# Gate and up products in a PSUM tile each: a two-layer hybrid trunk on one Trainium2 core

## The chip, the cores and the metric

The kernel runs on one core of a Trainium2 chip (trn2). The metric is the device time of one execution in microseconds, and the median of several executions is what is compared. The engines of the core are named as in the profile: PE (matrix products; PEld is its loading of stationary operands), DVE (VectorE), ACT (ScalarE), POOL (GpSimd) and SP, whose queue issues nearly all loads. Matrix products are accumulated in PSUM, from which ACT and DVE read.

## What is computed

Two layers run over 256 latent tokens and 256 context tokens of 1024 features in fp32. Each layer is a token mixer (two attentions and a convolution between an input and an output projection) followed by a mixture of experts; the second layer's mixture runs on the 256 latent tokens alone. The change lies in the experts:

```python
def hierarchical_moe(h, w_group, b_group, w_expert, b_expert, w_gate, w_up, w_down):
    # 32 experts in 4 groups; each token goes to 2 experts of one group
    ...
    def run(args):
        xb, e = args
        return (jax.nn.silu(xb @ w_gate[e]) * (xb @ w_up[e])) @ w_down[e]
    ...
```

with `w_gate` and `w_up` of 1024 x 512 and `w_down` of 512 x 1024 for each of 32 experts and each of two layers.

## The kernel before

**Experts.** A layer works through its 32 experts in 16 pairs, two of them to a quad `qd`. Each expert of a pair has 64 places for tokens, so that a pair fills the 128 PSUM partitions: expert `e` writes partitions 64e to 64e+63. `pair` (line 1344) does, in this order: 16 gate products (`m == 0`), the SiLU of their sum on ACT (`sil`, L1358), 16 up products (`m == 1`), the product of their sum with `sil` and the token weights on DVE (`act`, L1363), four transposes (`pat`), 16 down products into `py`, and `split_y`, which reads `py` in two halves: ACT rounds a half to `YH` (L1275), DVE subtracts to get the rest `YL` (L1276). In the second layer DVE first multiplies by a gate (`Yg`, L1273). The trace counts each of these fp32 products as two instructions, so its rows show 32 where the code has 16.

**Work between the products.** `burst(0)` stands between gate and up products, `burst(1)` behind `act`, `burst(2)` behind the transposes' copy, `burst(3)` amid the down products. They hold what belongs to neighbouring pairs: the return of the previous pair's rows to their tokens (`pc`, the "adders"), the gathering of the next quad's rows (`pg`) and its one-hot matrix `OH` (DVE, L1289). In the first layer, in all but the first and the last two pairs, `burst(0)` holds at most that one-hot matrix, which is no PE work. In the second layer it holds three adders from the second pair on.

**PSUM.** `ps2` has two places of two banks (2 x 512 fp32 for each partition), `ps1` four places of one bank. Before, a pair takes one place for gate and up together, `p[:, 0]` and `p[:, 1]`, and the other for `py`. A place is handed out in turn, and a program that orders instructions by what tiles they touch puts in the waits; it tracks whole tiles.

**Loads.** Weights come over SP's queue in loads of 1024 KB into a ring of eight slots: a pair needs twelve (four each for gate, up and down). A load waits on SP until the products that read its slot are done, so PE's progress sets when loads start. The first pairs of a layer read weights that were loaded during the mixer, and the last pair uses loads of half the size.

**Order.** SP's order is that of the code. PE, DVE and ACT follow the code in the expert pairs (`tc.manual_schedule`). In the second layer's mixer, between the two mixtures, a list scheduler that estimates durations for the whole program from its start chooses the order on PE and ACT, and on DVE in parts.

Of the kernel before, what the change touches and what calls it, by code (L numbers as in the profile page):

```python
# [14 lines left out]
AF = mybir.ActivationFunctionType  # L15
OP = mybir.AluOpType
# [20 lines left out]
def trunk(ctx: ExitStack, tc: tile.TileContext, t_in, rope, out, cfg):  # L37
    nc = tc.nc
    pe, ve, sc, gp, sp = nc.tensor, nc.vector, nc.scalar, nc.gpsimd, nc.sync
# [17 lines left out]
    def K2(name, shape=(128, 512), dt=F32, tag="t"):  # L57
        t = k2[tag].tile([shape[0], 256 if tag == "m" else 512], dt, tag="k2" + tag, name=name)
        n = int(np.prod(shape[1:]))
        t = t[:, :n]  # L60
        if len(shape) == 3:
            t = t.rearrange("p (a b) -> p a b", a=shape[1])
        elif len(shape) == 4:
            t = t.rearrange("p (a b c) -> p a b c", a=shape[1], b=shape[2])
        return t

    def P2(name, dt=F32):
        return ps2.tile([128, 2, 512], dt, tag="p2", name=name)

    def P1(name, dt=F32):  # L70
        return ps1.tile([128, 512], dt, tag="p1", name=name)
# [29 lines left out]
    def load_rows_two(srcs, name):  # L101

        vs = [slot(name).rearrange("p (k f) -> p k f", f=512) for _ in srcs]
        for b in range(2):
            for v, src in zip(vs, srcs):
                sp.dma_start(v[:, 2 * b:2 * b + 2], src[b] if isinstance(src, list) else src[:, 2 * b:2 * b + 2])
        return [lambda k, v=v: v[:, k] for v in vs]
# [104 lines left out]
    def sqrt_table(after):  # L212

        sc.activation(sm.tile([128, 1], F32, name="warm"), after[:, 0:1], AF.Sqrt, scale=0.0)
# [249 lines left out]
    def layer(l):  # L464
# [39 lines left out]
        if l > 0:  # L504
            ws = Splits(wKV, 512)
# [486 lines left out]
        def down_half(h, e, pr):  # L992
            return [wdown_d[l, 2 * pr + e][256 * a:256 * a + 256, 512 * h:512 * h + 512].rearrange("(p k) d -> p k d", k=2)
                    for a in range(2)]
# [3 lines left out]
        def weights_of(pr, m, a, e):  # L998
            return down(a, e, pr) if m == 2 else gate_up(m, a, e, pr)
# [242 lines left out]
        def row_adders(YH, YL, oht, new=P1):  # L1242

            def d_major(o):
                pc = new("pc")
                pe.matmul(pc, YH[:, 128 * o:128 * o + 128], oht, start=True, stop=False)  # L1246
                pe.matmul(pc, YL[:, 128 * o:128 * o + 128], oht, start=False, stop=True)  # L1247
                for s in range(2):
                    sl = slice(256 * s, 256 * s + 256)
                    ve.scalar_tensor_tensor(xT[:, o, sl], pc[:, sl], mod[l][:, 5, o, s:s + 1], xT[:, o, sl],  # L1250
                                            op0=OP.mult, op1=OP.add)

            def t_major(t, hf):
                pc = new("pc")
                o_, sl = oht[:, 128 * t:128 * t + 128], slice(512 * hf, 512 * hf + 512)
                pe.matmul(pc, o_, YH[:, sl], start=True, stop=False)  # L1256
                pe.matmul(pc, o_, YL[:, sl], start=False, stop=True)  # L1257
                ve.tensor_tensor(xo[t][:, sl], xo[t][:, sl], pc, op=OP.add)  # L1258

            if last:  # L1260
                return [lambda t=t, hf=hf: t_major(t, hf) for hf in range(2) for t in range(2)]
            return [lambda o=o: d_major(o) for o in range(KC)]

        def y_tiles():
            return K4("YH", (128, 1024), F32R), K4("YL", (128, 1024), F32R), K4("Yg") if last else None

        def split_y(py, h, rows, tiles):

            YH, YL, y = tiles
            sl = slice(512 * h, 512 * h + 512)  # L1270
            py = py[:rows]
            if last:
                ve.tensor_tensor(y[:rows, sl], py, g2r[:rows, sl], op=OP.mult)  # L1273
                py = y[:rows, sl]
            sc.copy(YH[:rows, sl], py)  # L1275
            ve.tensor_tensor(YL[:rows, sl], py, YH[:rows, sl].bitcast(F32), op=OP.subtract)  # L1276
# [59 lines left out]
        def weight(m, a, e, pr):  # L1336

            t = pre.pop((pr, m, a, e), None) or load_rows(weights_of(pr, m, a, e), "we")
            if not isinstance(t, list):
                return lambda k: t[:, k]  # L1340
            n = 1 if m == 2 else 2
            return lambda k: t[k // n][:, k % n]

        def pair(pr, xg, ws, burst, final, finish):


            p = P2("pgu")
            for m in range(2):
                for a in range(2):
                    w_ = (load_rows_two([weights_of(pr, m, a, e) for e in range(2)], "we") if final else  # L1350
                          [weight(m, a, e, pr) for e in range(2)])
                    for k in range(4 * a, 4 * a + 4):
                        for e in range(2):
                            pe.matmul(p[64 * e:64 * e + 64, m, :], xg[:, k, 64 * e:64 * e + 64], w_[e](k % 4),  # L1354
                                      start=k == 0, stop=k == KC - 1)
                if m == 0:
                    sil = K2("sil", tag="w")
                    sc.activation(sil, p[:, 0], AF.Silu)  # L1358
                    if final:
                        sqrt_table(sil)  # L1360
                    burst(0)
            act = K2("act", tag="w")
            ve.scalar_tensor_tensor(act, p[:, 1], ws, sil, op0=OP.mult, op1=OP.mult)  # L1363
            burst(1)
            pt = P1("pat")
            for f in range(4):
                pe.transpose(pt[:, 128 * f:128 * f + 128], act.rearrange("s (a p k) -> s a k p", a=2, k=2)[:, f // 2, f % 2], ident)  # L1367
            actT = K2("actT", tag="w")
            sc.copy(actT, pt)  # L1369
            burst(2)  # L1370
            tiles = y_tiles()
            oht = K2("oht", (128, 512), F32R)

            def slots():
                pb = P1("pb")
                se = sm.tile([32, 2, 64], F32R, name="se")
                gp.tensor_copy(se, ident[:32, 2 * pr:2 * pr + 2, None].to_broadcast([32, 2, 64]))  # L1377
                pe.matmul(pb[:, :N], se.rearrange("p a b -> p (a b)"), posT[:, :N], start=True, stop=True)  # L1378
                ve.tensor_scalar(oht[:, :N], pb[:, :N], slotid, None, op0=OP.is_equal)

            def products(py, wd, fs):
                for f in fs:
                    for e in range(2):
                        pe.matmul(py[64 * e:64 * e + 64, :], actT[:, 128 * f + 64 * e:128 * f + 64 * e + 64],  # L1384
                                  wd[e](f), start=f == 0, stop=f == 3)

            slots()
            if final:
                for h in range(2):
                    py = P2("py")[:, 0]  # L1390
                    wd = load_rows_two([down_half(h, e, pr) for e in range(2)], "we")
                    products(py, wd, range(2))
                    if h == 0:
                        burst(3)
                    else:
                        finish(0, tiles, oht[:, :N], py)
                    products(py, wd, range(2, 4))
                    if h == 0 or not last:
                        split_y(py, h, 128, tiles)
                finish(1, tiles, oht[:, :N], py)  # L1400
                return []
            py = P2("py")
            for a in range(2):
                wd = [weight(2, a, e, pr) for e in range(2)]
                for f in range(2 * a, 2 * a + 2):
                    for h in range(2):
                        for e in range(2):
                            pe.matmul(py[64 * e:64 * e + 64, h], actT[:, 128 * f + 64 * e:128 * f + 64 * e + 64],  # L1408
                                      wd[e](f % 2)[:, 512 * h:512 * h + 512], start=f == 0, stop=f == 3)
                if a == 0:  # L1410
                    burst(3)
            for h in range(2):
                split_y(py[:, h], h, 128, tiles)
            return row_adders(tiles[0], tiles[1], oht[:, :N])
# [183 lines left out]
        for qd in range(8):  # L1598
            nxt, steps, _ = quad(qd + 1) if qd < 7 and (qd or cfg["n0"]) else (None, [], None)
            for e in range(2):  # L1600
# [4 lines left out]
                with man():  # L1605
# [21 lines left out]
                    def burst(i):  # L1627
                        for f in at[i]:
                            f()
# [62 lines left out]
```

## Time and profile before

| | |
|---|---|
| Median of 3 executions | 1475.16 us (1473.77 to 1477.0) |
| The profiled execution, its own time | 1472.71 us |
| Its span, first to last instruction | 1470.7 us |
| Experts of the first layer | about 305 to 798 us |
| Mixer of the second layer | about 798 to 994 us |
| Experts of the second layer | about 994 to 1460 us |
| PE busy, share of the span | 95% |
| DVE, ACT busy | 42%, 27% |
| Moved from HBM | 479.42 MB, 327 GB/s over the span |

Times in rows are microseconds from the start of the span. "idle before" is how long the engine stood still ahead of an instruction, and the arrow names what ended that.

### The profile page before, as it was taken

The numbers are of one execution on the slowest core, as the hardware profiler recorded it, in microseconds if no ns is written. First come the engines' busy times: TensorE is split into PE (matmuls) and PEld (weight loads), VectorE is DVE, ScalarE is ACT, GpSimd is POOL, SyncE is SP. The second block draws the span as 40 slices with busy tenths as digits, with TensorE's granted clock in tenths as the row PEclk, the third lists the DMA queues.
The fourth block names the chain that finished last, engine by engine and source line by source line (L and its number), as shares of the span: only waits on it lengthen the run. The fifth ranks groups of instructions, "written<-read, shape, count | busy, mean of one in ns | idle before, by whom it ended". The sixth has DMA issues, their size and how long they took to land. (4 is left out here: it accounts for less than half of the span.)

```text
span 1470.7 us, 20485 instructions
## 1 busy us (share of the span) xinstructions
PE 1390.8 (95%) x8068; PEld 771.3 (52%) x8068; DVE 613.4 (42%) x1380; ACT 395.7 (27%) x954; POOL 76.7 (5%) x132
## 2 busy tenths in 40 slices
PE   6999999999999999999998998889999999999987
PEld 5776677755445544444434776783433343333332
DVE  4379974443323423233325679853222222222223
ACT  4454675421111111101102565552111011111102
POOL 1202000100000000000001110010000000000000
PEclk9999999999999999999999999999999999999999
DMA  9757204397999999999999590186999999999996
GB/s 350 282 166 284 109 1 172 131 375 306 376 408 414 413 400 406 417 406 414 385 405 389 201 332 31 44 357 280 388 422 421 421 421 421 421 421 419 421 417 255
DMA packets 97412, 481.86 MB, mean 328 GB/s; under 512 B 14068, under 2 KB 22544, under 8 KB 52128
## 3 DMA queue, kind: packets, MB, share of 16 engines
q1 hardware_dynamic: 96576, 478.79, 81.1%
q8 instruction: 66, 1.08, 0.3%
q10 hardware_dynamic: 464, 1.11, 0.2%
q0 software_dynamic: 272, 0.59, 0.1%
q14 instruction: 34, 0.28, 0.0%
HBM read 479.42 MB, written 1.05 MB: 327 GB/s over the span
## 5 line engine op out<-in xcount | busy, mean ns | idle before, releaser
L1354 PE MATMUL pgu<-we,xg 128*64 128x512 f32 x1904 | 449.3, 598 | 30.7 <-DMA we<-in_w_gate_dram 13.6
L1354 PEld LDWEIGHTS pgu<-we,xg 128*64 128x64 f32 x1904 | 142.3, 137 | 324.1 <-issue 246.8
L1408 PE MATMUL py<-we,actT 128*64 128x512 f32 x888 | 202.9, 596 | 0.7 <-ACT actT L1369 0.7
L1363 DVE SCALAR_TENSOR_TENSOR act<-pgu,ws,sil 128x512 f32<-128x512 f32 x32 | 24.0, 751 | 285.1 <-PE pgu L1354 248.6
L1250 DVE SCALAR_TENSOR_TENSOR xT<-pc,mod,xT 128x256 f32<-128x256 f32 x256 | 104.8, 477 | 52.9 <-PE pc L1247 52.2
L1408 PEld LDWEIGHTS py<-we,actT 128*64 128x64 f32 x888 | 63.1, 137 | 117.5 <-issue 113.4
L1304 ACT COPY xg<-pg 128x256 f32<-128x256 f32 x112 | 36.3, 376 | 308.2 <-PE pg L1300 308.2
L1258 DVE TENSOR_TENSOR xo<-xo,pc 128x512 f32<-128x512 f32 x62 | 39.8, 684 | 112.0 <-PE pc L1257 112.0
L1299 PE MATMUL pg<-OH,hH 128*128 128x256 f32 x336 | 83.3, 286 | 0.0
L1300 PE MATMUL pg<-OH,hL 128*128 128x256 f32 x336 | 82.1, 283 | 0.0
L643 DVE SCALAR_TENSOR_TENSOR ca<-gpad,cw,ca 128x512 f32<-128x512 f32 (+1 forms) x120 | 74.2, 619 | 0.9
L1299 PEld LDWEIGHTS pg<-OH,hH 128*128 128x128 f32 x336 | 63.9, 190 | 7.2 <-issue 5.7
L1300 PEld LDWEIGHTS pg<-OH,hL 128*128 128x128 f32 x336 | 64.1, 191 | 0.9
L1358 ACT ACTIVATE sil<-pgu 128x512 f32<-128x512 f32 x32 | 19.1, 598 | 167.6 <-PE pgu L1354 167.6
L281 PE MATMUL pm<-wm,scT 128*32 128x256 f32 (+1 forms) x896 | 60.7, 359 | 3.0 <-DMA wm<-in_w_mod_dram 2.8
L1273 DVE TENSOR_TENSOR Yg<-py,g2r 128x512 f32<-128x512 f32 x31 | 21.3, 688 | 100.7 <-PE py L1408 96.4
L1276 DVE TENSOR_TENSOR YL<-py,YH 128x512 fp32r<-128x512 f32 x32 | 22.1, 690 | 92.7 <-ACT YH L1275 92.7
L1275 ACT CAST YH<-Yg 128x512 fp32r<-128x512 f32 x31 | 19.1, 617 | 141.2 <-DVE Yg L1273 141.2
L1275 ACT CAST YH<-py 128x512 fp32r<-128x512 f32 x32 | 18.7, 585 | 139.0 <-PE py L1408 113.8
L1377 POOL CAST se<-ident 32x128 fp32r<-32x128 f32 x32 | 9.1, 287 | 900.1 <-PE pb L1378 900.1
L1246 PE MATMUL pc<-oht,YH 128*128 128x512 f32 x128 | 53.4, 418 | 1.2 <-ACT YH L1275 1.2
L1247 PE MATMUL pc<-oht,YL 128*128 128x512 f32 x128 | 50.6, 395 | 0.2 <-DVE YL L1276 0.2
(429 smaller groups left out, 2106.0 us busy)
## 6 DMA issues: line engine op xcount, KB each, us to landing
we<-in_w_up_dram SPq DMA_DIRECT2D x112, 1024.0 KB, 9.7
we<-in_w_down_dram SPq DMA_DIRECT2D x111, 1024.0 KB, 12.4
we<-in_w_gate_dram SPq DMA_DIRECT2D x110, 1024.0 KB, 13.5
wm<-in_w_mod_dram SPq DMA_DIRECT2D x44, 1024.0 KB, 9.4
wp<-in_w_gate_dram SPq DMA_DIRECT2D x8, 1024.0 KB, 9.5
wp<-in_w_up_dram SPq DMA_DIRECT2D x8, 1024.0 KB, 9.7
we<-in_w_gate_dram SPq DMA_DIRECT2D x16, 512.0 KB, 12.1
we<-in_w_up_dram SPq DMA_DIRECT2D x16, 512.0 KB, 10.2
```

What stands on the lines that cost most here:

```text
L281: pe.matmul(p[0][32 * q:32 * q + 32], scT[:, kq, :], ws[128 * kq // nr][:, kq % (nr // 128), c:c + n], start=k == 0, stop=k == KC * nq // ...
L643: ve.scalar_tensor_tensor(a, g, wt, a, op0=OP.mult, op1=OP.add)
L1246: pe.matmul(pc, YH[:, 128 * o:128 * o + 128], oht, start=True, stop=False)
L1247: pe.matmul(pc, YL[:, 128 * o:128 * o + 128], oht, start=False, stop=True)
L1250: ve.scalar_tensor_tensor(xT[:, o, sl], pc[:, sl], mod[l][:, 5, o, s:s + 1], xT[:, o, sl], op0=OP.mult, op1=OP.add)
L1258: ve.tensor_tensor(xo[t][:, sl], xo[t][:, sl], pc, op=OP.add)
L1275: sc.copy(YH[:rows, sl], py)
L1299: pe.matmul(dst, hH[t][:, 128 * k:128 * k + 128], rhs, start=t == 0, stop=False)
L1300: pe.matmul(dst, hL[t][:, 128 * k:128 * k + 128], rhs, start=False, stop=t == NT - 1)
L1304: sc.copy(xg[e][:, k - 1:k + 1, :], v[:, :, e])
L1354: pe.matmul(p[64 * e:64 * e + 64, m, :], xg[:, k, 64 * e:64 * e + 64], w_[e](k % 4), start=k == 0, stop=k == KC - 1)
L1408: pe.matmul(py[64 * e:64 * e + 64, h], actT[:, 128 * f + 64 * e:128 * f + 64 * e + 64], wd[e](f % 2)[:, 512 * h:512 * h + 512], start=f == ...
```

## The change

Gate and up products of a pair get a tile of `ps2` each, of which only the first bank is used, in place of the two banks of one tile. With `py` a pair now takes three tiles, and since there are two places, the three results of consecutive pairs take them by turns: gate in A, up in B, `py` in A, the next pair's gate in B, its up in A, its `py` in B. What a product waits for at its start is the reading of the tile that had its place before: a gate product's that of the previous pair's up result (`act`), an up product's that of the previous pair's `py` (`split_y`), a down product's that of its own pair's gate result (`sil`).

```diff
         def pair(pr, xg, ws, burst, final, finish):
 
 
-            p = P2("pgu")
             for m in range(2):
+                p = P2("pgu")[:, 0]
                 for a in range(2):
                     w_ = (load_rows_two([weights_of(pr, m, a, e) for e in range(2)], "we") if final else
                           [weight(m, a, e, pr) for e in range(2)])
                     for k in range(4 * a, 4 * a + 4):
                         for e in range(2):
-                            pe.matmul(p[64 * e:64 * e + 64, m, :], xg[:, k, 64 * e:64 * e + 64], w_[e](k % 4),
+                            pe.matmul(p[64 * e:64 * e + 64, :], xg[:, k, 64 * e:64 * e + 64], w_[e](k % 4),
                                       start=k == 0, stop=k == KC - 1)
                 if m == 0:
                     sil = K2("sil", tag="w")
-                    sc.activation(sil, p[:, 0], AF.Silu)
+                    sc.activation(sil, p, AF.Silu)
                     if final:
                         sqrt_table(sil)
                     burst(0)
             act = K2("act", tag="w")
-            ve.scalar_tensor_tensor(act, p[:, 1], ws, sil, op0=OP.mult, op1=OP.mult)
+            ve.scalar_tensor_tensor(act, p, ws, sil, op0=OP.mult, op1=OP.mult)
             burst(1)
```

On PE no product of the experts moves. What changes is what the first up product waits for. Here is that place in a pair of the first layer (the third row of the piece, in its two versions, is the first up product; DMAHW names a load, Activation is ACT):

```order
 L1354 MATMUL pgu<-we,xg 64x512 [waits DMAHW2_49]
 L1354 MATMUL pgu<-we,xg 64x512 x6
-L1354 MATMUL pgu<-we,xg 64x512 [waits DMAHW3_49,Activation_49]
+L1354 MATMUL pgu<-we,xg 64x512 [waits DMAHW3_49,DVE_49,PE_49]
 L1354 MATMUL pgu<-we,xg 64x512 [waits DMAHW4_49]
 L1354 MATMUL pgu<-we,xg 64x512 x6
```

The wait for ACT has gone, and waits for DVE (the reading of the previous `py`) and for PE's own earlier products have come.

The orders on SP and POOL stay. In the second layer's mixer, whose code the diff does not touch, the scheduler chooses another order on PE, ACT and DVE. On ACT, at the start of that mixer (`hT`: the modulated rows for the input projection, two instructions for each k; `wh`: rounding of its weights; `ms` and `mod`: a modulation vector), before:

```order
L352 COPY rs<-rb 128x512
L370 ACTIVATE hT<-hx,mod_224 128x256
L288 COPY ms<-pm 128x256
L370 ACTIVATE hT<-hx,mod_224 128x256 x3
L304 COPY mod_224<-pm 128x16
L370 ACTIVATE hT<-hx,mod_224 128x256 x2
L385 CAST wh<-wkv 128x512
```

and now:

```order
L352 COPY rs<-rb 128x512
L370 ACTIVATE hT<-hx,mod_224 128x256 x4
L288 COPY ms<-pm 128x256
L370 ACTIVATE hT<-hx,mod_224 128x256 x4
L304 COPY mod_224<-pm 128x16
L385 CAST wh<-wkv 128x512 x2
L370 ACTIVATE hT<-hx,mod_224 128x256
```

The copy `ms` moves behind three more `hT`, and two `wh` stand together. On DVE, at the end of that mixer's convolution (`ca`: a tap of the convolution; `ars`, `qT`: attention results; `wl`: the rest of the rounded weights; `csq`, `cn2v`, `cn2r`: the convolution's norm), before:

```order
L643 SCALAR_TENSOR_TENSOR ca<-gpad,cw,ca 128x256 x2
L387 TENSOR_TENSOR wl<-wo,wh 128x512
L643 SCALAR_TENSOR_TENSOR ca<-gpad,cw,ca 128x256 x2
L871 TENSOR_TENSOR ars<-po,ars 128x128
L786 TENSOR_TENSOR ca<-ca,cm 128x256 x2
L874 TENSOR_TENSOR qT<-ars,qT 128x128
L790 TENSOR_TENSOR csq<-csq,csq_8343 128x256
L330 TENSOR_SCALAR cn2v<-css 128x2
L387 TENSOR_TENSOR wl<-wo,wh 128x512
```

and now:

```order
L643 SCALAR_TENSOR_TENSOR ca<-gpad,cw,ca 128x256
L871 TENSOR_TENSOR ars<-po,ars 128x128
L387 TENSOR_TENSOR wl<-wo,wh 128x512
L874 TENSOR_TENSOR qT<-ars,qT 128x128
L786 TENSOR_TENSOR ca<-ca,cm 128x256 x2
L790 TENSOR_TENSOR csq<-csq,csq_8359 128x256
L387 TENSOR_TENSOR wl<-wo,wh 128x512
L330 TENSOR_SCALAR cn2v<-css 128x2
```

Three of the taps have moved to an earlier place in the mixer, and one `wl` stands ahead of `cn2v` in place of behind it.

## Rows read from the trace of the kernel before

**Rows 1.** The page of the profile: the span, PE's busy time, and what the loads moved in each of 40 slices of the span (about 37 us a slice).
```profile
span 1470.7 us, 20485 instructions
...
PE 1390.8 (95%) x8068; PEld 771.3 (52%) x8068; DVE 613.4 (42%) x1380; ACT 395.7 (27%) x954; POOL 76.7 (5%) x132
...
GB/s 350 282 166 284 109 1 172 131 375 306 376 408 414 413 400 406 417 406 414 385 405 389 201 332 31 44 357 280 388 422 421 421 421 421 421 421 419 421 417 255
```

**Rows 2.** PE's waits between 305 and 800 us (the first layer's experts), longest total first: total us, how often, the longest one.
```profile
PE pgu L1354 <- ACT sil L1358: 10.3, 13, 1.1
PE pgu L1354 <- DVEq L1454: 1.5, 1, 1.5
PE pc L1246 <- ACT YH L1275: 1.2, 1, 1.2
...
```

**Rows 3.** The timeline of all engines over one pair boundary of the first layer, from the down products of one pair to the first up products of the next: start, duration, engine, line, instruction, count. SPq is SP's queue issuing loads.
```profile
513.56 7.09 PE L1408 MATMUL py<-we,actT 128*64 128x512 f32 x32
...
517.24 4.24 SPq L98 DMA_DIRECT2D we<-in_w_up_dram  x4
520.48 7.04 PE L1354 MATMUL pgu<-we,xg 128*64 128x512 f32 x32
520.72 0.59 ACT L1275 CAST YH<-py 128x512 fp32r<-128x512 f32 x1 [8.21 <-PE py L1408]
...
522.07 0.59 ACT L1275 CAST YH<-py 128x512 fp32r<-128x512 f32 x1 [0.76 <-DVE YL L1276]
522.68 0.69 DVE L1276 TENSOR_TENSOR YL<-py,YH 128x512 fp32r<-128x512 f32 x1 [0.65 <-ACT YH L1275]
...
527.92 0.60 ACT L1358 ACTIVATE sil<-pgu 128x512 f32<-128x512 f32 x1 [5.27 <-PE pgu L1354]
528.58 0.65 PE L1354 MATMUL pgu<-we,xg 128*64 128x512 f32 x2 [1.06 <-ACT sil L1358]
```

**Rows 4.** PE's timeline: gate products (no wait) and up products (behind the wait) of three other pairs of the first layer; 397.21 and 644.03 are the gates of two pairs eight apart.
```profile
397.21 7.04 PE L1354 MATMUL pgu<-we,xg 128*64 128x512 f32 x32
405.03 7.09 PE L1354 MATMUL pgu<-we,xg 128*64 128x512 f32 x32 [0.78 <-ACT sil L1358]
...
551.13 7.04 PE L1354 MATMUL pgu<-we,xg 128*64 128x512 f32 x32
558.95 7.09 PE L1354 MATMUL pgu<-we,xg 128*64 128x512 f32 x32 [0.78 <-ACT sil L1358]
...
644.03 7.04 PE L1354 MATMUL pgu<-we,xg 128*64 128x512 f32 x32
```

**Rows 5.** DVE's timeline at the pair whose gate starts at 551.13: the last half of the split, late because a one-hot matrix went ahead of it.
```profile
553.74 0.68 DVE L1276 TENSOR_TENSOR YL<-py,YH 128x512 fp32r<-128x512 f32 x1
```

**Rows 6.** Two single microseconds of the pair boundary of rows 3: busy time of each engine, then PE's granted clock (1.00 is the upper level), the share of the 16 DMA engines' time, and GB/s.
```profile
517.00:518.00 1.00, 1.00 (x8) 0.38 (x6) 0.00 (x0) 0.00 (x0) 0.00 (x0) 1.00 0.59 246
518.00:519.00 1.00, 1.00 (x8) 0.33 (x6) 0.00 (x0) 0.00 (x0) 0.00 (x0) 1.00 0.73 147
```

**Rows 7.** The same columns for one stretch of 30 us in each layer's experts.
```profile
510.00:540.00 30.00, 28.94 (x148) 13.55 (x147) 8.59 (x20) 3.19 (x8) 0.29 (x1) 1.00 0.99 407
...
1210.00:1240.00 30.00, 28.38 (x129) 11.19 (x129) 7.29 (x14) 3.33 (x8) 0.29 (x1) 1.00 1.01 421
```

**Rows 8.** ACT's timeline: the SiLU of two pairs of the second layer that are six apart.
```profile
1138.28 0.60 ACT L1358 ACTIVATE sil<-pgu 128x512 f32<-128x512 f32 x1 [5.84 <-PE pgu L1354]
...
1318.12 0.60 ACT L1358 ACTIVATE sil<-pgu 128x512 f32<-128x512 f32 x1 [6.24 <-PE pgu L1354]
```

**Rows 9.** The loads issued between 500 and 560 us (two pairs): count, KB each, median us from issue to landing.
```profile
we<-in_w_gate_dram SPq DMA_DIRECT2D x8, 1024.0 KB, 13.7
we<-in_w_up_dram SPq DMA_DIRECT2D x8, 1024.0 KB, 7.7
we<-in_w_down_dram SPq DMA_DIRECT2D x8, 1024.0 KB, 10.7
```

**Rows 10.** PE's waits between 1000 and 1470 us (the second layer's experts), as rows 2.
```profile
PE pgu L1354 <- DMA we<-in_w_gate_dram: 13.6, 14, 1.3
PE pgu L1354 <- DMA we<-in_w_up_dram: 3.0, 11, 0.3
...
PE pgu L1354 <- ACT sil L1358: 0.2, 1, 0.2
```

**Rows 11.** PE's waits between 795 and 1000 us (the second layer's mixer), as rows 2, the longest three.
```profile
PE pqt L734 <- DVE tq L731: 3.3, 1, 3.3
PE cr L344 <- DVE cn2r L338: 2.5, 1, 2.5
PE pp L1204 <- DVE selb L1193: 2.4, 1, 2.4
...
```

**Rows 12.** The first stretch of that mixer, columns as in rows 6.
```profile
806.00:892.00 86.00, 85.19 (x627) 64.50 (x629) 59.57 (x139) 46.46 (x115) 13.33 (x18) 0.98 0.70 253
```

**Rows 13.** Four rows of timelines of that mixer: three of the `hT` on ACT, taps on DVE, `cn2v` on DVE, and the first load for the second layer's experts on SP's queue.
```profile
811.66 1.31 ACT L370 ACTIVATE hT<-hx,mod 128x256 fp32r<-128x256 f32 x3
...
896.89 2.04 DVE L643 SCALAR_TENSOR_TENSOR ca<-gpad,cw,ca 128x256 f32<-128x256 f32 x4
...
950.56 0.34 SPq L1021 DMA_DIRECT2D xs<-in_w_down_dram  x1
...
952.48 0.16 DVE L330 TENSOR_SCALAR cn2v<-css 128x2 f32<-128x2 f32 x1 [0.76 <-PE css L423]
```

## The prediction, made before the changed kernel was run

> **What bounds the kernel now.** I read the page first, to see where PE and the loads are full, then PE's waits by stage, then the timeline of one pair boundary, and last the loads by the microsecond. PE is busy 95% of the span, and in the two expert stages the loads run at 375 to 422 GB/s in nearly every slice [rows 1]. Two limits lie close together, so each layer has to be read by itself.
>
> In the first layer's experts PE waits 10.3 us, 13 times, for the SiLU on ACT, then 1.5 us once for a branch; no load is among its longest waits [rows 2]. PE sets the pace there. One boundary shows why: the down products start at 513.56 and the gate products at 520.48, 6.92 us for 32 instructions without a gap; the up products start at 528.58, 8.10 us after the gate products, behind an ACT instruction that reads the tile's other half [rows 3]. In the usual pair it is 7.82 us (397.21 to 405.03, 551.13 to 558.95) with 0.78 us shown as idle [rows 4]. So a wait costs 7.82 - 6.92 = 0.90 us, 0.12 more than the idle that the profile shows, since the pipeline also drains. The period of a pair is (644.03 - 397.21) / 8 = 30.85 us [rows 4].
>
> In the second layer's experts PE waits 13.6 and 3.0 us for loads and 0.2 us for the SiLU, once [rows 10]: three adders stand between gate and up and hide it. The loads set the pace, with 421 GB/s [rows 7] and a period of (1318.12 - 1138.28) / 6 = 29.97 us [rows 8].
>
> **The change, part by part.**
>
> The wait removed: an up product no longer waits for `sil`, as its tile is another one. 13 waits of 10.3 us in all [rows 2], and 0.12 us of drain for each: 10.3 + 13 x 0.12 = 11.9 us. In the second layer it removes 0.2 us from PE, at a place where the first pair's weights are there already; I count it at nothing, since the loads set the end of that stage (if I am wrong, it is 0.2 us more).
>
> The wait added on up: it now waits for the split of the previous pair's `py`. In rows 3 the last `YL` ends at 522.68 + 0.69 = 523.37, 2.9 us after the gate products began; at the pair with a one-hot matrix ahead of it, 553.74 + 0.68 = 554.42, 3.3 us after 551.13 [rows 4, 5]. The gate products take 6.92 us, so 3.6 us are spare and the wait costs nothing. Without that cover (a split that ended only with the gate products) each further microsecond would cost a microsecond for each of the 13 pairs. Behind the waiting up product stand all PE's later products, so there is no way round it.
>
> The waits added on gate and down: gate waits for the previous `act`, down for its own pair's `sil`. The `sil` of rows 3 starts at 527.92 and is over some 15 us before that pair's down products (its up products alone take 7 us and the bursts follow); `act` lies a whole set of down products (6.92 us) ahead of the next gate. Nothing for both.
>
> What the loads then allow: a pair reads 12 loads of 1024 KB, 12.58 MB, or 29.9 us at 421 GB/s; the second layer, paced by its loads, does it in 29.97 [rows 8]. PE's new period in the first layer is 30.85 less 0.93 (the mean over these 8 pairs: seven of 0.90, one of 1.18) = 29.92 us. The two limits meet. Can the loads give this? Today the queue runs dry once a pair: up loads are issued at 517.24, when the down products have freed their slots [rows 3], and in the two microseconds from 517 the rate is 246 and 147 GB/s, in place of 421 [rows 6]: (175 + 274) / 421 = 1.07 us of a pair are lost. That is the room which the faster PE uses. The stock ahead of PE: the four up loads of a pair come in two groups, 7.7 us being their median to landing [rows 9]; issued at 517.24 and about 521, the second group lands about 529 and is needed halfway through the up products, near 527.5 + 3.5 = 531. That leaves about 2 us. If the loads lag by 29.97 - 29.92 = 0.05 us a pair, nine pairs use up 0.5 us of it. So I take the full gain up to the last pairs. There the half-size loads follow without a dry stretch, and the gain of the last of the 13 pairs (0.9 us) may go to a wait for them. Lower bound of this term: 11.9 - 0.5 - 0.9 = 10.5; upper bound 11.9; I take 11.3, nearer the upper, since rows 2 show no wait for a load at all today.
>
> A rule stands against this. The Trainium skill, in "TensorE: Matmul & The Clock Gate", section "HAM oscillation — how this bites in real kernels", reports a kernel whose products wait for transfers, and in which double buffering of PSUM "gave no further gain". By it the sum would be about nothing. The second layer here is that case (its row shows 0.2 us to win); the first, where PE waits for ACT and not for loads, is not.
>
> The order in the second layer's mixer: the scheduler sees the pairs end at other times and lays out about 200 us anew. Same instructions, same loads. On ACT `ms` stands behind three more `hT`, 1.31 us [rows 13]; PE meanwhile has products without a gap, 85.19 us of 86 [rows 12], which cover it; without the cover it would cost 1.3. On DVE three taps (2.04 us for four, so about 1.5 us) move away from the end of the convolution, whose norm PE waits 2.5 us for today [rows 11, 13]; a gain of up to 1.5 us at that place, paid for by attention steps that come as much later. `wl` ahead of `cn2v` lies in 0.76 us in which DVE waits for PE [rows 13]. Bounds: a loss of 1.3 + 1.5 = 2.8, a gain of 2.5 (the wait for the norm); I take 0.
>
> What carries it to the end: the first load of the second layer's experts is issued at 950.56, during that mixer [rows 13], and waits for attention's end; so the loads that pace the second layer start as much earlier as the mixer does, and what the first layer wins arrives whole.
>
> Sum: 1472.7 (the profiled execution's own time, 2.4 us under the median of the runs) - 11.3 = 1461.4; on the median 1475.2 - 11.3 = 1463.9 us, 0.77% faster.
>
> **The rivals.**
>
> (a) The loads don't give more in the first layer than they do now. For: 407 GB/s at a DMA share of 0.99 [rows 7], hence 12.58 / 407 = 30.9 us a pair, the present period. Against: the dry stretch of rows 6, and 421 in the second layer. Then only the first three pairs gain, which read preloaded weights: 3 x 0.9 = 2.7 us, 1472.5. It would show as waits of PE for up loads. This is the case in which the rule above would hold.
>
> (b) The mixer's new order costs 3 to 8 us. For: PE waits there for DVE and ACT in turn [rows 11], and its granted clock is not at the upper level all the time (mean 0.98) [rows 12]. Against: unchanged work and its long gapless stretch. Time 1467 to 1472, around 1469.
>
> (c) Slower: the split comes late, and up waits longer for DVE than it did for ACT. It decides once the last `YL` ends over 6.92 + 0.90 = 7.8 us after the gate's start, where it is 2.9 to 3.3 now. If the split of some 2.9 us ran only behind the gate products, up would start after 9.8 us in place of 7.8: 2.0 us for 15 pairs of the first layer, 30 us, 1505. Against: ACT and DVE are idle for 5 us ahead of `sil` [rows 3].
>
> (d) The wait doesn't go, since another wait on ACT stands in the same place: 1475. Against: the order of waits in the changed program.
>
> **How the numbers follow.** The forecast 0.72, (a) 0.10, (b) 0.11, (c) 0.03, (d) 0.04. The forecast's own range: gains of 10.5 - 2.8 to 11.9 + 2.5, that is 1460.8 to 1467.5. The range of 8 in 10 reaches into (b): 1460 to 1470. Within 0.2% (3 us, which is about what the spread of the three runs, 1473.77 to 1477.0, lets one tell) lie (d) and half of (a), with the far end of (b): 0.10. Faster 0.87, slower 0.03.
>
> **What would show it.** PE's waits for `sil` in the first layer gone, gate to up 6.92 us, period of a pair near 29.9; the dry microsecond on the queue gone or nearly so; PE's waits for up loads in the first layer under 1 us in all; the second layer's experts begin 11 us earlier and last as long as now. Wrong it would be if PE's waits for loads in the first layer came to several us (a), or if the mixer, 196 us from 798 to 994 now, grew by over 3 us (b).

## The result, and the profile after

The changed kernel takes 1461.99 us (median; 1460.91 to 1463.18), the kernel before on the same chip 1474.47 us (1472.77 to 1477.0). The ratio is 0.9912, 95% interval 0.9896 to 0.9928: 0.88% faster. The two profiled executions are 1472.71 and 1461.98 us, 10.7 us apart.

The page after, rows answering to [rows 1]: as many products, the loads of the second layer's experts at 421 GB/s as before, and in slices 12 to 21, the first layer's experts, 403 to 423 GB/s where it was 385 to 417.

```profile
span 1459.9 us, 20482 instructions
...
PE 1391.9 (95%) x8068; PEld 778.6 (53%) x8068; DVE 612.2 (42%) x1380; ACT 395.3 (27%) x954; POOL 78.1 (5%) x132
...
GB/s 352 281 161 290 117 2 151 130 378 315 389 419 415 420 416 416 423 416 420 403 413 388 175 340 1 105 328 289 389 422 421 422 420 422 421 421 420 421 417 255
```

PE's waits between 305 and 800 us after the change, the counterpart of [rows 2]. The 13 waits for `sil` are gone; the branch's 1.5 us is now the longest, and still no load stands in the list.

```profile
PE pgu L1354 <- DVEq L1454: 1.5, 1, 1.5
PE ss L423 <- ACT sq L417: 1.4, 1, 1.4
PE pc L1246 <- ACT YH L1275: 1.2, 1, 1.2
PE pat L1367 <- DVE act L1363: 0.8, 2, 0.6
```

PE's timeline gives the starts that are summed below: the gate products of the second pair, of two pairs eight apart, of the last pair of the first layer, and of the first pair of the second layer.

```profile
330.66 0.60 PE L1354 MATMUL pgu<-we,xg 128*64 128x512 f32 x2
...
395.01 1.46 PE L1354 MATMUL pgu<-we,xg 128*64 128x512 f32 x6
...
636.36 1.03 PE L1354 MATMUL pgu<-we,xg 128*64 128x512 f32 x4
...
754.53 1.03 PE L1354 MATMUL pgu<-we,xg 128*64 128x512 f32 x4
...
983.83 0.65 PE L1354 MATMUL pgu<-wp,xg 128*64 128x512 f32 x2
```

From them the period is (636.36 - 395.01) / 8 = 30.17 us, where it was 30.85. Cut into stages, before and after:

| stage | before, us | after, us | difference |
|---|---|---|---|
| start to the second pair's gate, first layer | 330.92 | 330.66 | -0.3 |
| 14 pairs, to the last pair's gate | 433.96 | 423.87 | -10.1 |
| last pair and the second layer's mixer | 229.41 | 229.30 | -0.1 |
| second layer's experts to the end | 476.41 | 476.07 | -0.3 |

So nearly the whole difference, 10.1 of 10.8 us, lies in the pairs of the first layer. It should have been larger: the 13 waits were counted at 11.9 us. The rest is seen on PE's weight loads (PEld), in rows of each kernel's list of waits between 305 and 800 us, before and then after.

```profile
PEld pgu L1354 <- ACT sil L1358: 21.8, 13, 1.9
...
PEld pgu L1354 <- DMA we<-in_w_up_dram: 1.1, 3, 0.6
```
```profile
PEld pgu L1354 <- DMA we<-in_w_up_dram: 3.0, 8, 0.7
```

Before, the weight loads waited for the Silu, and for up loads only in the last pair (776 to 780 us), whose loads are of half size. Now they wait for up loads in five earlier pairs too, two of them here:

```profile
435.34 2.34 PEld L1354 LDWEIGHTS pgu<-we,xg 128*64 128x64 f32 x13 [0.38 <-DMA we<-in_w_up_dram]
...
495.83 0.20 PEld L1354 LDWEIGHTS pgu<-we,xg 128*64 128x64 f32 x4 [0.68 <-DMA we<-in_w_up_dram]
```

They are too short to show as idle time of the products, whose ends are modelled, but they show in the length of an unbroken run of 64 gate and up products, 13.96 us in one pair and 14.33 in the next. In eight of the 14 pairs, the five with a named wait among them, this run is longer than the 13.90 us that it takes undisturbed (13.95 behind the branch), by 0.06 to 0.87 us and by 3.2 us in all.

```profile
515.84 13.96 PE L1354 MATMUL pgu<-we,xg 128*64 128x512 f32 x64
...
545.26 14.33 PE L1354 MATMUL pgu<-we,xg 128*64 128x512 f32 x64
```

The split has ended well before the up products, as [rows 3, 5] had it: in the pair of 545.26 with the one-hot matrix ahead of it, the last `YL` ends at 548.54, 3.3 us after the gate's start.

```profile
547.86 0.68 DVE L1276 TENSOR_TENSOR YL<-py,YH 128x512 fp32r<-128x512 f32 x1
```

The loads, with the columns of [rows 6] and [rows 7]. The dry stretch of the pair boundary is shallower, ((421 - 320) + (421 - 311)) / 421 = 0.5 us lost in place of 1.07, and over 30 us the rate is 415 GB/s in place of 407.

```profile
513.00:514.00 1.00, 1.00 (x7) 0.29 (x4) 0.00 (x0) 0.00 (x0) 0.00 (x0) 1.00 1.12 320
514.00:515.00 1.00, 1.00 (x8) 0.30 (x6) 0.00 (x0) 0.00 (x0) 0.00 (x0) 1.00 0.76 311
```
```profile
510.00:540.00 30.00, 30.00 (x153) 14.74 (x151) 9.83 (x22) 3.65 (x8) 0.28 (x1) 1.00 1.01 415
```

The second layer waits for loads as before, the counterpart of [rows 10]; and the first load for it is issued at 938.40 in place of 950.56 [rows 13].

```profile
PE pgu L1354 <- DMA we<-in_w_gate_dram: 14.1, 14, 1.3
PE pgu L1354 <- DMA we<-in_w_up_dram: 2.9, 11, 0.3
```
```profile
938.40 0.34 SPq L1021 DMA_DIRECT2D xs<-in_w_down_dram  x1
```

### The profile page after: what moved, and what is told of

It is laid out like the page before. It is cut to its first block, busy times and chain, and to the rows that moved or that the text cites. A ratio compares the mean times of both kernels' runs of the same rounds, so it can differ in the third digit from the quotient of the medians.

```text
span 1459.9 us, 20482 instructions
## 1 busy us (share of the span) xinstructions
PE 1391.9 (95%) x8068; PEld 778.6 (53%) x8068; DVE 612.2 (42%) x1380; ACT 395.3 (27%) x954; POOL 78.1 (5%) x132
## 5 line engine op out<-in xcount | busy, mean ns | idle before, releaser
L1354 PEld LDWEIGHTS pgu<-we,xg 128*64 128x64 f32 x1904 | 147.7, 137 | 307.8 <-issue 242.0
## 6 DMA issues: line engine op xcount, KB each, us to landing
we<-in_w_up_dram SPq DMA_DIRECT2D x16, 512.0 KB, 10.2
```

The costliest lines, as they stand in the source:

```text
L1354: pe.matmul(p[64 * e:64 * e + 64, :], xg[:, k, 64 * e:64 * e + 64], w_[e](k % 4), start=k == 0, stop=k == KC - 1)
```

## The experiments

Runs are read by stage, since the start alone moves a run's time: with the 8 places for loads the first gate product of the first layer came between 305.3 and 308.6 us in the profiled executions. "Ratio" is that to the kernel before in the same comparison; "14 pairs", "period", "mixer" (with the last pair) and "second" are the stages above, from each run's own timeline. The stage of 14 pairs repeats well from one profiled kernel to another: 433.96 to 434.27 us where only the old wait is in it (before, e2, e8, e11), 423.23 to 423.96 us with the change and all loads (after, e1, e6, e9).

| kernel | median us | ratio, 95% | 14 pairs | period | mixer | second |
|---|---|---|---|---|---|---|
| before | 1474.47 | 1 | 433.96 | 30.85 | 229.41 | 476.4 |
| after | 1461.99 | 0.9912 (0.9896 to 0.9928) | 423.87 | 30.17 | 229.30 | 476.1 |
| e1 | 1462.44 | 0.992 (0.9899 to 0.9941) | 423.89 | 30.22 | 228.53 | 476.2 |
| e2 | 1474.44 | 0.9999 (0.9987 to 1.001) | 434.27 | 30.85 | 232.36 | 476.1 |
| e3 | 1468.53 | 0.9963 (0.9946 to 0.998) | 429.25 | 30.17 | 227.93 | 476.2 |
| e4 | 1465.32 | 0.9934 (0.991 to 0.9958) | 425.64 | 30.17 | 228.39 | 475.9 |
| e5 | 1485.19 | 1.006 (1.004 to 1.0081) | 441.20 | 31.38 | 231.74 | 476.1 |
| e6 | 1462.13 | 0.9915 (0.9894 to 0.9937) | 423.23 | 30.09 | 228.55 | 475.9 |
| e7 | 1460.52 | 0.9902 (0.9884 to 0.992) | 420.63 | 29.81 | 229.18 | 475.9 |
| e8 | 1471.61 | 0.9968 (0.9953 to 0.9984) | 434.02 | 30.85 | 227.87 | 476.0 |
| e9 | 1466.5 | 0.9943 (0.9927 to 0.9959) | 423.96 | 30.16 | 232.61 | 476.0 |
| e10 | 1486.43 | 1.0079 (1.0055 to 1.0104) | 437.81 | 30.85 | 239.50 | 475.9 |
| e11 | 1482.53 | 1.0047 (1.0027 to 1.0067) | 434.04 | 30.85 | 238.45 | 476.5 |
| e12 | 1481.56 | 1.0047 (1.003 to 1.0065) | 440.65 | 31.54 | 229.70 | 478.4 |

**Which layer: e1 and e2.** The change in one layer alone.

```
+            apart = l == 0            (e2: l == 1)
+            both = None if apart else P2("pgu")
             for m in range(2):
-                p = P2("pgu")[:, 0]
+                p = P2("pgu")[:, 0] if apart else both[:, m]
```

> Separate gate and up tiles in the first layer alone; the second layer keeps the tile of both. Theory: the whole change is the PE's wait for the gate's Silu at 13 pairs of the first layer, so the experts of the first layer should take 10.0 us less than before and all else nothing, 1461 to 1464.5 us in all. Rival (the freer places also help in the second layer, or the mixer's new order is a part of the gain): 1466 us or more, with the first layer's experts less than 9 us shorter.

> Separate tiles in the second layer alone. Theory: there the Silu is already done when the up products come, since three adders stand between them, and the PE waits for loads: 1472 to 1477 us, no difference from before. Rival (a part of the gain is the second layer's): 1 to 5 us less than before.

Both came as the theory had it: e1 has the whole gain (its 14 pairs 423.89 us), e2 none (0.9999). The profiled e2 spent 3 us more in the mixer; it is the slowest of e2's ten executions, whose median is that of before.

**Is it the wait: e3 and e4.** Two adders between the gate and the up products of the first layer.

```
-                        at = [mine[:hot], head + a_[:2] + g[:2] + a_[2:4],
+                        at = [mine[:hot] + a_[:2], head + g[:2] + a_[2:4],
```

> The kernel before, with its tile of both. In the first layer the first two adders of the previous pair stand between the gate and the up products instead of behind the up products, so that the PE has some 1 us of work while the Silu runs. Theory (the gain is the hidden Silu, however it is hidden): the wait of 0.79 us a pair goes and the layer is as fast as with separate tiles, 1461 to 1465 us. Rival (what helps is three results taking two places by turns, not the wait): 1472 to 1477 us, as before.

> The changed kernel with the same two adders moved between gate and up. Theory: there is nothing left to hide, 1461 to 1464 us, as the changed kernel. Rival (the gate and up products of a pair still lose something at their boundary in the changed kernel): 2 us or more less than the changed kernel. If the adders meet a late split there, some us more.

e3, the tile of both kept: PE's products no longer wait for `sil` and the period falls from 30.85 to 30.17 us. So the gain is the hidden Silu, not the turn of the three results. The time fell only half as far as expected: in the 14 pairs e3 is 429.25 - 423.87 = 5.4 us behind the changed kernel. Of that, 3.6 us is one pair behind the branch, 34.99 us long (31.38 in e4), with an idle stretch in its gate products in which the profile shows nothing that PE waited for, and a lower granted clock (0.73 on average) behind it. PE's timeline, then a window with the columns of [rows 6]:

```profile
671.15 2.79 PE L1354 MATMUL pgu<-we,xg 128*64 128x512 f32 x11 [1.50 <-DVEq L1454]
675.93 6.63 PE L1354 MATMUL pgu<-we,xg 128*64 128x512 f32 x21 [2.00 <-issue]
```
```profile
675.00:680.00 5.00, 4.07 (x14) 1.35 (x16) 0.00 (x0) 0.00 (x0) 0.00 (x0) 0.73 0.99 380
```

What caused that idle stretch stays open; e3's ten times run from 1463.6 to 1474.3 us. Its other 13 pairs are as long as e4's within 0.02 us, so the remaining 1.8 us is what e4 loses too.

e4 gained nothing, and lost 1.8 us in its pairs: moved adders have a price of their own, 30.17 - 29.81 = 0.36 us a pair over the changed kernel with loads out of its way (e7, below). Two of e4's rows of waits on weight loads show it: the first up weights wait for the last adder, 0.37 us each time, and waits for loads are down to 1.0 us.

```profile
PEld pgu L1354 <- PE pc L1247: 5.5, 15, 0.4
...
PEld pgu L1354 <- DMA we<-in_w_up_dram: 1.0, 2, 0.8
```

In e3 the profile puts the same wait of the weight loads down to `sil`, but the up products start 8.1 us after the gate products in e3 and e4 alike, so that the Silu is not what holds them.

```profile
PEld pgu L1354 <- ACT sil L1358: 4.7, 13, 0.4
```

So the period of 30.17 us in e3 and e4 equals the changed kernel's by coincidence: PE with the moved adders here, the loads there.

**A later Silu: e5 and e6.** A copy of the gate products ahead of the Silu, in the kernel before (e5) and after (e6).

```
+                    if not last:
+                        sc.copy(sil, p[:, 0])      (e6: p)
                     sc.activation(sil, p[:, 0], AF.Silu)
```

> The kernel before, with a copy of the gate products (128x512, about 0.6 us on ACT) ahead of each Silu of the first layer, written to the place that the Silu writes again. Theory: each of the 13 waits of the PE before the up products grows from 0.79 us by the copy's 0.6 us, and every pair's period with it: 13 to 15 times 0.6 = 8 to 9 us slower than before, 1481 to 1485 us. Rival (the loads pace the layer and the wait is mostly hidden by them): under 3 us slower.

> The changed kernel with the same copy ahead of each Silu of the first layer. Theory: the Silu now has the whole up run (some 7 us) to end in, and the copy's 0.6 us is hidden: 1461 to 1465 us, the pair's period 30.2 us as without it. Rival (a wait for the Silu is left somewhere in the changed kernel): 3 us or more slower than the changed kernel.

e6 hides the copy whole. e5 pays 0.53 us a pair, 7.2 us in 14 pairs; the median is 10.5 us up. Its first pair adds to that: the copy there stands ahead of ACT's table load, so the up products start at 318.15, some 2.6 us after the gate products (PE idle for 1.64 of them), and run 8.78 us where they took 7.09, at a granted clock of 0.72 on average. ACT, PE, and a window of e5:

```profile
315.60 0.59 ACT L1359 COPY sil<-pgu 128x512 f32<-128x512 f32 x1 [4.76 <-PE pgu L1354]
316.20 1.28 ACT L1360 ACT_TABLE_LOAD   x1
317.50 0.60 ACT L1360 ACTIVATE sil<-pgu 128x512 f32<-128x512 f32 x1
```
```profile
310.16 5.37 PE L1354 MATMUL pgu<-wp,xg 128*64 128x512 f32 x24
318.15 8.78 PE L1354 MATMUL pgu<-wp,xg 128*64 128x512 f32 x32 [1.64 <-ACT sil L1360]
```
```profile
320.00:325.00 5.00, 5.00 (x18) 1.45 (x16) 0.00 (x0) 0.00 (x0) 0.00 (x0) 0.72 0.78 315
```

**What the loads take back: e7 and e8.** One load in twelve left out in pairs 2 to 14 of the first layer, counted from 0; the products take the first expert's up weights in its place, so the result is another.

```
+                          [weight(m, a, 0, pr)] * 2 if not last and m and a and pr > 1 else
                           [weight(m, a, e, pr) for e in range(2)])
```

> The changed kernel, but in pairs 2 to 14 of the first layer the second expert's lower half of the up weights is not loaded, and the products take the first expert's tile in its place (so the result is another): 11 loads of 1 MB a pair in place of 12. Theory (since the change the loads take back a part of the gain): the PE's short waits for up loads in the first layer (3.0 us on its weight loads) go, the pair's period falls from 30.17 to 29.9 us or a little less, and the kernel is 2 to 4 us faster than the changed one, 1458 to 1460.5 us. Rival (the PE's own work makes the 30.17): period 30.17, 1461 to 1464 us.

> The kernel before with the same load left out (11 loads a pair, another result). Theory: before the change no load holds the PE in the first layer, so the period stays 30.85 us and the time that of before, 1472 to 1477 us. Rival (loads pace the layer already before): 2 us or more faster.

This pair gives the sizes, from one profiled execution each. With loads out of the way the change is worth 434.02 - 420.63 = 13.4 us in the 14 pairs, and the loads take 423.87 - 420.63 = 3.2 us of it back in the changed kernel, as much as its longer runs of 64 products sum to; they take nothing from the kernel before in these pairs (434.02 against 433.96). e7 as a whole is 1.5 us faster than the changed kernel, less than 3.2, its start being 1.7 us later. The times of e8 lie 3 us below those of before although its 14 pairs last as long. In the last pair the up products lose to loads in either kernel (7.90 us before, 7.98 after, 7.09 in e7 and e8), which is 0.8 us of e8's 3; the rest stays open, and by their medians e7 and e8 are only 11.1 us apart. e7's 64 gate and up products run 13.90 us without a load in their way:

```profile
545.28 13.90 PE L1355 MATMUL pgu<-we,xg 128*64 128x512 f32 x64
559.12 1.05 PE L1325 MATMUL pw<-whl,OH 128*128 128x4 f32 x8
```

To the next instruction that is 559.12 - 545.28 = 13.84 us. In the kernel before the same stretch is 565.97 - 551.13 = 14.84, of which the up products are 565.97 - 558.95 = 7.02:

```profile
565.97 1.05 PE L1325 MATMUL pw<-whl,OH 128*128 128x4 f32 x8
```

So one wait costs 1.00 us: 0.95 up to the start of the up products (7.82 us, in place of the 6.87 us after which e7's trace has the 33rd of the 64 products), and 0.05 more in their run (7.02 in place of 6.97).

**The new wait: e9, e10, e11.** The subtraction that makes YL done 3 times (e9) or 6 times (e10) over in the changed kernel, and 6 times in the kernel before (e11).

```
+            for _ in range(1 if last else 3):      (e10, e11: 6)
                 ve.tensor_tensor(YL[:rows, sl], py, YH[:rows, sl].bitcast(F32), op=OP.subtract)
```

> The changed kernel; in the first layer the DVE's subtraction that makes YL (128x512, 0.69 us) is done three times over for each half, so that the split of a pair's result ends 2.8 us later, some 5.7 us after the next gate run's start. Theory (the new wait of the up run is on this split, with 3.6 us to spare of a gate run of 6.92 us): nothing, 1461 to 1465 us, and no wait of the PE on YL before the up products. Rival (less to spare than counted): 5 us or more.

> The changed kernel with the subtraction done six times over: the split ends 6.9 us later, some 9.8 us after the gate run's start. Theory: at 14 pairs of the first layer the up run now waits 2.9 to 3.4 us for YL, 35 to 48 us more than the changed kernel, 1497 to 1510 us. Rival (no such dependence, or it is hidden by the loads): 1461 to 1466 us.

> The kernel before with the subtraction done six times over. Theory: there the place that the split holds is taken next by the results of the next pair, some 20 us later, and the adders that read YL stand behind the up run: 1472 to 1478 us, as before. Rival (a late split costs in either kernel, by way of DVE's order or of the adders): 10 us or more slower.

In the pairs e9 costs nothing (423.96 us): the up products have that much to spare, and little more. In a pair with a one-hot matrix ahead of the split, whose gate starts at 547.09, the last YL ends at 551.75 + 2.14 = 553.89, 6.8 us later.

```profile
551.75 2.14 DVE L1277 TENSOR_TENSOR YL<-py,YH 128x512 fp32r<-128x512 f32 x3 [0.65 <-ACT YH L1275]
```

By the medians e9 takes 4.5 us more than the changed kernel, by the profiled executions 4.8: their stages differ by 3.3 us behind the pairs, at the last pair, whose adders wait for YL with nothing beside them, and by 1.7 us at the start. I had left the last pair out of all three expectations. One row of PE's waits to 810 us, of e9 and of e11:

```profile
PE pc L1247 <- DVE YL L1277: 2.4, 2, 1.7
```
```profile
PE pc L1247 <- DVE YL L1277: 6.8, 2, 3.9
```

In e11 the 14 pairs are as before (434.04), and the excess again lies at the end of the layer (238.45 against 229.41). e10 is the surprise. The split ends 11 us after the gate's start, and yet the up products start after 7.8 us, behind the Silu, and the period is 30.85 us, that of the kernel before:

```profile
550.55 7.04 PE L1355 MATMUL pgu<-we,xg 128*64 128x512 f32 x32
558.37 1.94 PE L1355 MATMUL pgu<-we,xg 128*64 128x512 f32 x8 [0.78 <-ACT sil L1359]
```
```profile
557.39 4.32 DVE L1277 TENSOR_TENSOR YL<-py,YH 128x512 fp32r<-128x512 f32 x6 [0.65 <-ACT YH L1275]
```

So the two places are not handed out strictly in turn, as the section on the kernel before has it. In the built program of the changed kernel they do come by turns. In that of e10 the up tile of 13 of the 14 pairs lies in the same place as the gate tile of its pair. This fits a program that is laid out along its own estimate of times, in which a new tile gets the place that comes free first; the places show the outcome, while the reason is argued. In those 13 pairs a late split costs the old wait and no more.

In two pairs, the one behind the branch and the last of the layer, e10's up tile is in the place of the previous `py`, and there the wait that I had meant shows. Behind the branch the last YL ends at 681.56 + 4.32 = 685.88 and the up products start at 685.98, 10.5 us after the gate's start, 2.7 us more than behind a Silu. In the last pair it ends at 773.99 + 4.32 = 778.31 and they start at 778.40, 10.2 us after the gate's start, 1.7 us more than in the changed kernel. The profile names no releaser for either stop, only "issue", and e3's idle stretch behind the branch has that name without a late YL; that it is the YL here is read from the times, 0.10 and 0.09 us apart, and from the places.

```profile
681.56 4.32 DVE L1277 TENSOR_TENSOR YL<-py,YH 128x512 fp32r<-128x512 f32 x6 [0.65 <-ACT YH L1275]
...
773.99 4.32 DVE L1277 TENSOR_TENSOR YL<-py,YH 128x512 fp32r<-128x512 f32 x6 [0.65 <-ACT YH L1275]
```
```profile
675.49 7.09 PE L1355 MATMUL pgu<-we,xg 128*64 128x512 f32 x32 [1.50 <-DVEq L1455]
685.98 4.49 PE L1355 MATMUL pgu<-we,xg 128*64 128x512 f32 x12 [3.40 <-issue]
...
778.40 7.09 PE L1355 MATMUL pgu<-we,xg 128*64 128x512 f32 x32 [1.62 <-issue]
```

**Stock of loads: e12.** `"ring": 7` in place of 8 in the changed kernel.

> The changed kernel with 7 in place of 8 places of 1 MB for weights in flight. Theory (what the loads take back in the first layer is a matter of stock: the transfers stop when no place is free, while the PE adds and gathers, and are late after it): the pair's period in the first layer grows from 30.17 us by 0.3 to 1.5 us, with more waits for loads on the PE, 5 to 25 us slower in all, the second layer's share included. Rival (only the mean rate of the loads counts): period 30.1 to 30.3 us, within 3 us of the changed kernel.

As the theory had it: period 31.54 us, longer than before the change with 8 places, 391 GB/s over 30 us, and PE now waits visibly for up loads.

```profile
PE pgu L1354 <- DMA we<-in_w_up_dram: 7.1, 11, 1.4
```
```profile
510.00:540.00 30.00, 28.59 (x137) 12.42 (x136) 7.25 (x16) 3.01 (x7) 0.28 (x1) 1.00 0.95 391
```

A version faster than the changed kernel with all its loads did not come out of this; e7 bounds what the loads could still give in the 14 pairs of the first layer at 3.2 us.

## Why the prediction held, point by point

**The wait removed.** Right in place and cause (e1, e3, e5 with e6). Its size was too small: put at 11.9 us, it is 13.4 with loads out of the way (e7 against e8). Most of the missing part is 0.10 us a wait. The step from gate to up products without a wait was taken from the down products, 6.92 us, and is 6.87; and the up products run slower behind a wait, 7.02 us in place of 6.97, which the gap between two starts does not contain.

**The loads.** This is the term that was mis-sized: put at a loss of 0.6 us (of at most 1.4: 0.5 for lag, 0.9 for the last of the 13 pairs), it is 3.2 us. The two limits do meet, as said, but PE's own new period is 29.81 us (e7), not 29.92, and with its loads it is 30.17, not the 29.97 of the second layer: 12.58 MB in 30.17 us are 417 GB/s. That the queue still has dry stretches in this layer, where all places are full while PE adds and gathers, fits the rows at 513 us and e12, but is argued. The pair in which I expected the loss had none; it is spread over eight pairs before it. "About 2 us of stock" was counted for one pair boundary; the run of 64 products already loses 14.33 - 13.90 = 0.4 us in single pairs. The sign that I named, under 1 us of PE's waits for up loads, came only to the letter: PE's list has none, but the waits of its weight loads came to 3.0 us (1.1 of it there before, which [rows 2], a list of products, don't show), and even these show less than e7. Rival (a) was thus true in part: the loads do give more (403 to 423 GB/s in place of 385 to 417), but not all that PE could take. The errors of these two terms have opposite signs, so it is in part luck that 13.4 - 3.2 = 10.2 stands so near the 11.3 of the forecast.

**The new wait on the split.** Nothing in the 14 pairs, as said (e9, which uses up nearly all of the time to spare: the split ends 6.8 us after a gate's start, the up products start after 6.9). But rival (c) was priced wrongly: 30 us and 1505 did not come of a far later split (e10, 1486.43 us), since it moved the up tile back to its old place in 13 of the 14 pairs, where the loss is that of the wait removed.

**The mixer and the way to the end.** 229.41 and 229.30 us, the norm's wait 2.5 to 2.0 us; the second layer's experts last as long and begin 10.5 us earlier. Rival (b) did not come. That the Silu's wait plays no part in the second layer is e2; there the case is near that of the rule quoted in the prediction from the Trainium skill ("TensorE: Matmul & The Clock Gate", "HAM oscillation — how this bites in real kernels"; the page says it of a version in which the waits for transfers had been gathered), and the ratio of 0.9999 agrees with it. The first layer before the change, where PE waited for ACT, is not.

**The whole.** 1461.99 us against 1463.9 forecast. The profiled executions differ by 10.7 us, the medians by 12.5; the 1.8 between are within the spread of the kernel before (1471.3 to 1477.9 over the comparisons here).

## What to carry to other kernels

Where an engine waits once a pair for another that reads half of its tile, a tile each removes the wait, and so does other work placed in the gap, if it has no switching price of its own. Before counting such a gain whole, ask what period the loads allow with the places they have, and prove it by leaving one load out: here it split 13.4 us of gain from 3.2 us that the loads took back. Short waits for loads don't always show as idle products; look at the weight loads' waits and at the length of an unbroken run.

## What the runs showed of the hardware that was not expected

After PE stood still between products for 1.64 us in e5, 2.00 us in e3 and 3.40 us in e10, its granted clock fell: 0.72 on average in the window of e5 from 320 us, 0.73 in that of e3 from 675 us, and 0.66 in e10 from 686 us, behind the 3.40 us shown above. 1.00 is the upper level (2.4 GHz); a single microsecond in e10's window reads 0.50, the lower one (1.2 GHz).

```profile
686.00:691.00 5.00, 5.00 (x16) 1.91 (x18) 0.00 (x0) 0.00 (x0) 0.00 (x0) 0.66 1.02 426
...
687.00:688.00 1.00, 1.00 (x4) 0.30 (x2) 0.00 (x0) 0.00 (x0) 0.00 (x0) 0.50 1.03 434
```

In e5 this made the up products of one pair 8.78 - 7.09 = 1.7 us longer, on top of the wait itself. The length of a stop alone does not decide it. In e9's second layer the clock stayed at 1.00 behind 2.39 us, and in e10 the products behind the 1.62 us shown above took their usual 7.09 us. e9's timeline and window:

```profile
1335.29 7.53 PE L1355 MATMUL pgu<-we,xg 128*64 128x512 f32 x32 [2.39 <-DVEq L1455]
```
```profile
1335.00:1340.00 5.00, 4.71 (x21) 1.69 (x23) 1.42 (x3) 0.62 (x1) 0.00 (x0) 1.00 1.03 423
```

Behind the waits of about 0.8 us that the change removes, the clock of the kernel before stayed at 1.00 in its window [rows 7].
